# Operand slots of 4608 bytes with gaps, and matmuls row by row in the middle chunks

## The chip, the cores and the metric

One core of a Trainium2 chip runs one step of a decoder layer. The time is what the device needs for one execution, in microseconds (us). The engines are named as the profile names them: PE multiplies matrices (PEld is its loading of the stationary operand), DVE and ACT work element by element, POOL does a few element operations, SP issues the transfers.

## The reference

264 tokens (8 single decode tokens and a prompt of 256) go through one layer of width 2048:

```python
proj = rmsnorm(x) @ w_in          # 2048 -> 6144, split into u, v, q, k, v, g
out  = concat(u * spatial_mix(v), silu(g) * groupnorm(retention(q, k, v))) @ w_out
h = x + out
h = h + softmax(q @ mem_k.T) @ mem_v @ w_co     # q = rmsnorm(h) @ w_cq, 4 heads, 256 memory tokens
h = h + square(relu(rmsnorm(h) @ w_ff1)) @ w_ff2   # 2048 -> 8192 -> 2048
y = rmsnorm(h)
```

All of it is float32. The memory keys and values of the prompt are two more products (256 memory tokens by w_ck and w_cv), and the decode tokens attend to cached keys and values that are read from memory.

## The kernel before, in words

**Layout.** Activations lie transposed: 128 features down the partitions, the 264 tokens along them. A tile of four such blocks, [128, 4, 264], is a slot (`slot`, L46). All slots come from one pool of 26 equal buffers. A block of 264 tokens has 1056 bytes per partition, which is 4 x 256 + 32; a slot has 4 x 1056 = 4224 bytes, which is 16 x 256 + 128. In the built program the pool begins at byte 73,664 = 287 x 256 + 192 of the partition. I call the byte at which an operand begins, modulo 256, its **residue**. So a slot begins at residue 192 or 64, its four blocks follow in steps of 32, and before the change all eight multiples of 32 occur as residues.

**The product.** A float32 operand is split into a rounded part and the rest (`split`, L98; the activations' pairs are `xh`/`xl`, `h1h`/`h1l`, `rh`/`rl` and so on, made by `pair`, L502; the weights' are `wh`/`wl`). One product of 128 features by 128 outputs is then three matmuls (L152 to L154): `wh` with the high part, `wh` with the low part, `wl` with the high part. The weights are the stationary operand, and the 264 tokens of one block move through. I call such three matmuls a **turn**. A turn is named by m, which of four groups of 128 outputs and so which bank of the accumulator it goes to, and by k, which of two blocks of features.

**The stream.** The weights come as 512 chunks of 256 x 512 numbers in a fixed order (L979 to L1018). Each chunk is loaded (L1024), rounded on ACT (L1030) and subtracted on DVE (L1038), some two chunks ahead of its matmuls. `group_act` (L136) makes 476 of the chunks: 444 with 264 columns and 32 with 256 (the memory keys, L999). A group of 16 blocks has 8 chunks; one of the feed-forward's second product has 4. A chunk has 8 turns, so 24 matmuls. Their order is by m first: both k for one bank, then the next bank. Only the first three chunks (FINE) go by k first. `group_mem` (L163, 32 chunks, the memory values) has the weights as the moving operand, 512 columns; `group_last` (L110) is the last group of four chunks.

**Other work.** Everything else (norms, attention, gating) is written as generators that are advanced a step at a time between turns (`run_point`, L210), so it stands in the engines' queues in that order. In the attention of the decode tokens (L806) DVE multiplies a cached key or value by a broadcast query and adds up (L822, L845); the product itself goes to a scratch tile of the pool `half` (L58) that nobody reads, in turn one of three buffers.

Of the kernel before, what the change touches and what calls it, by code (L numbers as in the profile page):

```python
# [6 lines left out]
F32 = mybir.dt.float32  # L7
F32R = mybir.dt.float32r
# [4 lines left out]
T = 264  # L13
TOK = ((8, 128), (136, 128), (0, 8))
EPS = 1e-6
NSLOT = 26
# [4 lines left out]
FINE = 3  # L21
# [4 lines left out]
G_N1, G_SGU, G_GN, G_N2, G_MEM, G_N3, G_FIN = 0, 16, 24, 32, 48, 64, 80  # L26
GAMMA = [1.0 - 2.0 ** (-5 - h) for h in range(8)]
R4 = range(4)


def build(tc, I, O):
    cst = tc.tile_pool(name="cst", bufs=1)
    wpool = tc.tile_pool(name="wpool", bufs=1)
    spool = tc.tile_pool(name="spool", bufs=1)
    tpool = tc.tile_pool(name="tpool", bufs=1)
    psum = tc.tile_pool(name="psum", bufs=1, space=bass.MemoryType.PSUM)
    with cst as cst, wpool as wpool, spool as spool, tpool as tpool, psum as psum:
        with tc.manual_schedule():
            _emit(tc, cst, wpool, spool, tpool, psum, I, O)


def _emit(tc, cst, wpool, spool, tpool, psum, I, O):
# [3 lines left out]
    def slot(shape, name, dt=F32):  # L46
        return spool.tile(shape, dt, name=name, tag="s", bufs=NSLOT)

    def t264(name="t"):
        return tpool.tile([128, T], F32, name=name, tag="t", bufs=9)  # L50

# [4 lines left out]
        return tpool.tile([128, n], F32, name=name, tag="sm", bufs=24)  # L56

    def half(name, dt=F32):  # L58
        return tpool.tile([128, 512], dt, name=name, tag="hf", bufs=3)

    def bank(shape, name):
        return psum.tile(shape, F32, name=name, tag="mm", bufs=5)
# [4 lines left out]
    S = {}  # L67
# [6 lines left out]
        S.pop(key)  # L74
        S.pop(key + "_cm").__exit__(None, None, None)

# [1 line left out]
    cmat = cst.tile([128, 272], F32, name="cmat")  # L78
    ident, trilt = cmat[:, 0:128], cmat[:, 128:256]
    kdec = cmat[:, 256:272]  # L80
# [3 lines left out]
    sel = cst.tile([128, 8], F32R, name="sel")  # L84
# [3 lines left out]
    def gain(base, k):  # L88
        return gcol[:, base + k:base + k + 1]
# [8 lines left out]
    def split(hi, lo, src, scale=None):  # L98
        if scale is None:
            act.copy(hi, src)  # L100
            dve.tensor_tensor(out=lo, in0=src, in1=hi.bitcast(F32), op=ALU.subtract)
        else:
            act.activation(hi, src, AF.Copy, scale=scale)  # L103
            dve.scalar_tensor_tensor(out=lo, in0=src, scalar=scale, in1=hi.bitcast(F32),  # L104
                                     op0=ALU.mult, op1=ALU.subtract)

# [1 line left out]
    chunks, started = [], []  # L108

    def group_last(w, opnd, evict):  # L110
# [25 lines left out]
    def group_act(w, nk, opnd, evict, pre=None, rot=0, n=T):  # L136
        st = {}

        def mm(ci, hi, lo):
            if ci == 0:  # L140
                st["ps"] = [bank([128, n], "acc") for _ in R4]
            turns = [(m, k) for m in R4 for k in range(2)]
            if len(started) < FINE:
                started.append(1)
                turns.sort(key=lambda t: t[1])
            for j, (m, k) in enumerate(turns):
                i = 2 * ci + k
                xh, xl = opnd((i + rot) % nk)
                a = hi[:, k, m * 128:(m + 1) * 128]
                b = lo[:, k, m * 128:(m + 1) * 128]  # L150
                ps = st["ps"][m][:]
                pe.matmul(ps, lhsT=a, rhs=xh, start=(i == 0), stop=False)  # L152
                pe.matmul(ps, lhsT=a, rhs=xl, start=False, stop=False)  # L153
                pe.matmul(ps, lhsT=b, rhs=xh, start=False, stop=(i == nk - 1))  # L154
                if j % 2:
                    yield

        for ci in range(nk // 2):
            chunks.append(dict(
                src=w[(ci + rot // 2) % (nk // 2)], mm=mm, ci=ci, pre=pre[ci] if pre and ci in pre else None,  # L160
                post=(lambda: evict(st["ps"])) if ci == nk // 2 - 1 else None))
# [20 lines left out]
            chunks.append(dict(src=w[ci], mm=mm, ci=ci, pre=None,  # L182
                               post=(lambda: evict(st["ps"])) if ci == 7 else None))

# [1 line left out]
    tasks, chains = [], []  # L186
    stores = deque()
    now = [0]
# [41 lines left out]
            now[0] += 1  # L230
            run_point()

# [1 line left out]
    class Stats:  # L234
        def __init__(self, n=T):
            self.n = n
            self.acc = tpool.tile([128, n], F32, name="sq", tag="sq", bufs=2)
            self.first, self.tail, self.ps = True, None, None
# [63 lines left out]
    def opnd_of(tiles):  # L302
        return lambda kt: (tiles[kt // 4][0][:, kt % 4, :], tiles[kt // 4][1][:, kt % 4, :])

# [1 line left out]
    open_pool("rpool")  # L306
    dve.memset(ones[:, 0:128], 1.0 / 2048)
    dve.memset(ones[:, 128:256], 1.0)
# [17 lines left out]

    keep_warm(NWARM)

    A = [(slot([128, 4, T], "xh", F32R), slot([128, 4, T], "xl", F32R)) for _ in R4]
    st1 = Stats()  # L330

    def prep_x(s, ks=R4):
# [52 lines left out]
        dve.tensor_scalar(out=tab[:, 2:4, :], in0=tab[:, 0:2, :], scalar1=128.0 ** -0.5, scalar2=None, op0=ALU.mult)  # L385
        S["tab"] = tab

# [1 line left out]
    def normed(ps):  # L389
        z = [t264("z") for _ in R4]  # L390
        for m in R4:
# [108 lines left out]
            dve.tensor_tensor(out=dst[1][:, m, :], in0=src[m][:], in1=dst[0][:, m, :].bitcast(F32), op=ALU.subtract)  # L500

    def pair(name):  # L502
        return slot([128, 4, T], name + "h", F32R), slot([128, 4, T], name + "l", F32R)

    def ev_u(g):
        def ev(ps):
# [10 lines left out]
            chain(gen())  # L517
        return ev

# [1 line left out]
    def ev_rope(which, g):  # L521
        def ev(ps):
            o = slot([128, 4, T], which)
# [156 lines left out]
            chain(gen())  # L680
        return ev

# [1 line left out]
    def ev_res(g, dst, st, gbase, name):  # L684
        def ev(ps):
            if g == 0:
# [20 lines left out]
            chain(gen())  # L707
        return ev

# [1 line left out]
    memop = []  # L711

    def mem_load(s):
# [4 lines left out]
    def mem_prep():  # L718
        st = Stats(256)
        nxt = mem_load(0)  # L720
        yield 6
        for s in R4:
            t = nxt
            if s < 3:
                nxt = mem_load(s + 1)
            mh, ml = slot([128, 4, 256], "memh", F32R), slot([128, 4, 256], "meml", F32R)
            memop.append((mh, ml))
            for k in R4:
                split(mh[:, k, :], ml[:, k, :], t[:, k, :], gain(G_MEM, 4 * s + k))
                q = st.square(t[:, k, :])  # L730
                yield 2
                st.add(q)

        def fin():
            tok = ((0, 128), (128, 128))
            st.column(tok)
            yield 4
            S["rsmb"] = cst.tile([128, 256], F32, name="rsmb")
            st.spread(S["rsmb"][:], tok)
            S["rsm"] = st.col  # L740
        defer(fin(), 10, front=True)
# [14 lines left out]
    def ev_cq(h):  # L756
        def ev(ps):
            if h == 0:
                zt = half("zt")
                dve.memset(zt[:], 0.0)  # L760
                S["qs"] = S["mpool"].tile([128, 512], F32R, name="qs", tag="qs", bufs=1)
                S["pst"] = S["mpool"].tile([128, 256], F32R, name="pst", tag="pst", bufs=1)
                act.copy(S["qs"][:], zt[:])
                act.copy(S["pst"][:], zt[:, 0:256])
                kv_fill()
            z = [t264("z") for _ in R4]
            for m in R4:
                dve.tensor_tensor(out=z[m][:], in0=ps[m][:], in1=S["st2r"][:], op=ALU.mult)
            qh, ql = pair("q")
            qx.append((qh, ql))  # L770
            small8 = S["mpool"].tile([128, 4, 8], F32, name="q8", tag="q8", bufs=4)
            q8.append(small8)

            def gen():
                for m in R4:
                    act.copy(small8[:, m, :], z[m][:, 0:8])
                    act.copy(qh[:, m, :], z[m][:])
                yield 4
                for m in R4:
                    gp.tensor_tensor(out=ql[:, m, :], in0=z[m][:], in1=qh[:, m, :].bitcast(F32), op=ALU.subtract)  # L780
            chain(gen())
            defer(sample_attn(h), 4, lane="kv")
        return ev

    def join_o(h):
        if h in oT and h in oS:
            oh, ol = oT[h]
            split(oh[:, :, 0:8], ol[:, :, 0:8], oS[h][:])

    def softmax(s, n, then=None):  # L790
        mx, nb, sm, rc = small(1, "mx"), small(1, "nb"), small(1, "sm"), small(1, "rc")
# [12 lines left out]
        return ex  # L804

    def sample_attn(h):  # L806
        qs, pst = S["qs"], S["pst"]
        tp = misc([8, 512], "tp")
        for m in R4:
            transpose(tp[:, m * 128:(m + 1) * 128], q8[h][:, m, :])  # L810
# [27 lines left out]
        for b in range(8):  # L838
            kv_fill()
            vc = kvq.popleft()  # L840
            pb = misc([128, 256], "pb")
            pe.matmul(pb[:], lhsT=sel[:, b:b + 1].broadcast_to([128, 128]), rhs=pst[:], start=True, stop=True)
            for d in R4:
                jk = half("vjk")
                dve.scalar_tensor_tensor(out=jk[:, 0:256], in0=vc[:, d * 256:(d + 1) * 256], scalar=1.0, in1=pb[:],  # L845
                                         op0=ALU.mult, op1=ALU.mult, accum_out=so[:, d, b:b + 1])
            yield 4
            kv_fill()
# [72 lines left out]
            split(oh[:, d, 8:T], ol[:, d, 8:T], op[:])  # L921
            yield 2

# [1 line left out]
    ffb = {}  # L925

    def ev_ff1(b, g):
# [48 lines left out]
            S["st4"].tail = t  # L976
            act.activation(S["gh"][3], h, AF.Copy, scale=gain(G_FIN, 15))

# [1 line left out]
    order = [("q", 2048), ("k", 3072), ("v", 4096), ("q", 2560), ("k", 3584), ("v", 4608),  # L980
             ("vA", 1024), ("vA", 1536), ("g", 5120), ("g", 5632), ("u", 0), ("u", 512)]
    seen = {}
# [13 lines left out]
        group_act(I["w_cq"][g], 16, opnd_of(opc), ev_cq(g))  # L996
    n_cq = len(chunks)
    for h in R4:
        group_act(I["w_ck"][h], 16, opnd_of(memop), ev_mk(h), n=256)  # L999
        group_mem(I["w_cv"][h], opnd_of(memop), ev_mv(h))  # L1000
    n_mem = len(chunks)
    for g in R4:
        group_act(I["w_co"][g], 16, opnd_of(oT), ev_res(g, opd, "st3", G_N3, "h2"))
# [206 lines left out]
```

## Time and profile before

| | |
|---|---|
| time, median of 3 runs | 1607.97 us (1607.68 to 1608.06) |
| span of the profiled execution, first to last instruction | 1605.7 us |
| PE busy | 1589.0 us, 12608 matmuls |
| DVE busy | 1049.4 us |
| ACT busy | 743.9 us |
| POOL busy | 146.5 us |
| transfers | 326.15 MB, DMA engines busy 59.2% on the queue that carries them |

The profiled execution has no time of its own beside its span; the median of the runs is 2.3 us above that span, which is what lies before the first and behind the last instruction. Matmuls are pipelined, so the duration of one overlaps the next; what counts for the time is the distance from the start of one to the start of the next. The timeline gives starts to 0.01 us.

### The profile page before, as it was taken

The numbers are of one execution on the slowest core, as the hardware profiler recorded it, in microseconds if no ns is written. First come the engines' busy times: TensorE is split into PE (matmuls) and PEld (weight loads), VectorE is DVE, ScalarE is ACT, GpSimd is POOL, SyncE is SP. The second block draws the span as 40 slices with busy tenths as digits, with TensorE's granted clock in tenths as the row PEclk, the third lists the DMA queues.
The fourth block names the chain that finished last, engine by engine and source line by source line (L and its number), as shares of the span: only waits on it lengthen the run. The fifth ranks groups of instructions, "written<-read, shape, count | busy, mean of one in ns | idle before, by whom it ended". The sixth has DMA issues, their size and how long they took to land.

```text
span 1605.7 us, 31031 instructions
## 1 busy us (share of the span) xinstructions
PE 1589.0 (99%) x12608; PEld 1560.8 (97%) x12608; DVE 1049.4 (65%) x1897; ACT 743.9 (46%) x1156; POOL 146.5 (9%) x138
## 2 busy tenths in 40 slices
PE   8999999999999999999999999999999999999997
PEld 7999999999999998999999999999999999999997
DVE  8758688678668777877655554554655555565555
ACT  5445466357444444444545443534444353444432
POOL 7403022010012111001000000000000000000000
PEclk9999999999999999999999999999999999999999
DMA  7565655455578887877555555455555555555552
GB/s 262 184 224 197 218 175 194 143 189 208 192 250 284 311 311 284 275 277 255 177 184 175 180 171 196 172 182 186 172 186 171 195 172 186 182 180 187 172 185 80
DMA packets 94222, 326.15 MB, mean 203 GB/s; under 512 B 10608, under 2 KB 15344, under 8 KB 94080
## 3 DMA queue, kind: packets, MB, share of 16 engines
q1 hardware_dynamic: 94080, 324.18, 59.2%
q8 instruction: 98, 1.61, 0.4%
q14 instruction: 44, 0.36, 0.1%
HBM read 313.03 MB, written 11.11 MB: 202 GB/s over the span
## 4 chain that ended last, share of the span: by engine, by line
PE 96%; DVE 2%; DMA 0%; issue 0%; ACT 0%; SPq 0%; POOL 0%; DVEq 0%; ACTq 0%
PE acc L152 28%; PE acc L153 28%; PE acc L154 28%; PE acc L176 2%; PE acc L178 2%; PE acc L177 2%; PE tp L96 1%; DVE wl L1038 1%; PE qb L819 0%; DMA hT<-in_xT_dram 0%; PE bc L618 0%; DVE xl L104 0%; PE spp L482 0%; DVE y L1121 0%; PE rsb L290 0%
## 5 line engine op out<-in xcount | busy, mean ns | idle before, releaser
L1030 ACT CAST wh<-w 128x1024 fp32r<-128x1024 f32 (+1 forms) x513 | 536.3, 1046 | 721.6 <-PE acc L153 638.7
L1038 DVE TENSOR_TENSOR wl<-w,wh 128x1024 fp32r<-128x1024 f32 (+1 forms) x513 | 631.2, 1243 | 255.1 <-ACT wh L1030 254.4
L152 PE MATMUL acc<-h2h,wh 128*128 128x264 f32 x1024 | 291.1, 284 | 0.0
L153 PE MATMUL acc<-h2l,wh 128*128 128x264 f32 x1024 | 291.0, 284 | 0.0
L154 PE MATMUL acc<-h2h,wl 128*128 128x264 f32 x1024 | 290.9, 284 | 0.0
L153 PE MATMUL acc<-rl,wh 128*128 128x264 f32 x992 | 282.3, 285 | 0.0
L154 PE MATMUL acc<-rh,wl 128*128 128x264 f32 x992 | 282.1, 284 | 0.0
L152 PE MATMUL acc<-rh,wh 128*128 128x264 f32 x992 | 282.1, 284 | 0.0
L152 PE MATMUL acc<-xh,wh 128*128 128x264 f32 x768 | 225.4, 293 | 0.2
L154 PE MATMUL acc<-xh,wl 128*128 128x264 f32 x768 | 219.9, 286 | 3.5 <-DVE wl L1038 2.9
L153 PE MATMUL acc<-xl,wh 128*128 128x264 f32 x768 | 219.6, 286 | 0.0
L152 PEld LDWEIGHTS acc<-h2h,wh 128*128 128x128 f32 x1024 | 192.9, 188 | 0.0
L153 PEld LDWEIGHTS acc<-h2l,wh 128*128 128x128 f32 x1024 | 192.8, 188 | 0.0
L154 PEld LDWEIGHTS acc<-h2h,wl 128*128 128x128 f32 x1024 | 192.6, 188 | 0.0
L152 PEld LDWEIGHTS acc<-rh,wh 128*128 128x128 f32 x992 | 187.0, 189 | 0.0
L153 PEld LDWEIGHTS acc<-rl,wh 128*128 128x128 f32 x992 | 186.8, 188 | 0.0
L154 PEld LDWEIGHTS acc<-rh,wl 128*128 128x128 f32 x992 | 186.5, 188 | 0.0
L154 PEld LDWEIGHTS acc<-xh,wl 128*128 128x128 f32 x768 | 145.7, 190 | 4.4 <-DVE wl L1038 3.7
L152 PEld LDWEIGHTS acc<-xh,wh 128*128 128x128 f32 x768 | 145.7, 190 | 1.9 <-ACT xh L103 0.7
L153 PEld LDWEIGHTS acc<-xl,wh 128*128 128x128 f32 x768 | 145.8, 190 | 0.2 <-DVE xl L104 0.2
L950 DVE TENSOR_TENSOR hT<-hT,acc 128x264 f32<-128x264 f32 x124 | 53.3, 430 | 73.4 <-PE acc L154 73.4
L92 POOL TENSOR_TENSOR msr<-msv,neghalf 128x3 f32<-128x3 f32 (+1 forms) x5 | 7.8, 1551 | 944.9 <-DVE msv L265 738.6
(255 smaller groups left out, 2800.0 us busy)
## 6 DMA issues: line engine op xcount, KB each, us to landing
w<-in_w_ff_dram SPq DMA_DIRECT2D x256, 512.0 KB, 4.1
w<-in_w_in_dram SPq DMA_DIRECT2D x95, 512.0 KB, 3.9
w<-in_w_out_dram SPq DMA_DIRECT2D x32, 512.0 KB, 4.1
w<-in_w_cq_dram SPq DMA_DIRECT2D x32, 512.0 KB, 4.2
kv<-in_kN_dram SPq DMA_DIRECT2D x32, 512.0 KB, 4.9
kv<-in_vT_dram SPq DMA_DIRECT2D x32, 512.0 KB, 5.2
w<-in_w_ck_dram SPq DMA_DIRECT2D x32, 512.0 KB, 5.3
w<-in_w_cv_dram SPq DMA_DIRECT2D x32, 512.0 KB, 4.4
```

Of the source, the lines that this page charges most:

```text
L92: gp.tensor_tensor(out=out, in0=in_, in1=neghalf[0:in_.shape[0], 0:n], op=ALU.pow)
L96: pe.transpose(out, in_, ident[0:p, 0:p])
L152: pe.matmul(ps, lhsT=a, rhs=xh, start=(i == 0), stop=False)
L153: pe.matmul(ps, lhsT=a, rhs=xl, start=False, stop=False)
L154: pe.matmul(ps, lhsT=b, rhs=xh, start=False, stop=(i == nk - 1))
L176: pe.matmul(ps, lhsT=a, rhs=hi[:, k, :], start=(kt == 0), stop=False)
L177: pe.matmul(ps, lhsT=a, rhs=lo[:, k, :], start=False, stop=False)
L178: pe.matmul(ps, lhsT=b, rhs=hi[:, k, :], start=False, stop=(kt == 15))
L950: dve.tensor_tensor(out=h[m], in0=h[m], in1=ps[m][:], op=ALU.add)
L1030: act.copy(hi[:, k, :], raws[i][:, k, :])
L1038: dve.tensor_tensor(out=lo[:, k, :], in0=raw[:, k, :], in1=hi[:, k, :].bitcast(F32), op=ALU.subtract)
```

## The change

It has two parts and some room-making.

**Slots.** A slot becomes 4608 bytes (18 x 256). Tiles that are moving operands of `group_act` are now made by `rows`: the tile is [128, 2, 576], two stretches of 2304 bytes (9 x 256), each holding two blocks of 264 tokens one behind the other with 48 numbers unused. The class `Rows` shows it to the rest of the kernel under the old indices. A tile of 96 bytes is put ahead of the slots, so that they begin at 73,664 + 96 = 288 x 256 + 32. Every even block then has residue 32 and every odd one 64, in all these slots. The memory operands (256 columns) take the same form. Other tiles in slots (the residual, the memory values, the keys of the prompt's attention) keep their shapes.

**Order.** In the chunks of a group that are neither its first nor its last, the turns go by k first: four banks with one block, then four banks with the other. Which block is first alternates from chunk to chunk, so that one chunk ends and the next begins with the same k. In the first and last chunk of a group the order stays by m, with the two k swapped for every second m. The flags that open and close an accumulation follow.

**Room.** The slots need 26 x 384 + 96 bytes more. `half` goes from three buffers to one, and the tile `pst` (the spread probabilities) is gone: it now lies in the first half of `qs`.

```diff
+class Rows:
+    def __init__(self, t):
+        self.v = t[:, :, 0:2 * T].rearrange("p a (b t) -> p a b t", b=2)
+    def __getitem__(self, at):
+        p, k, c = at
+        if isinstance(k, int):
+            return self.v[p, k // 2, k % 2, c]
+        return self.v[p, :, :, c]
...
+    spool.tile([128, 24], F32, name="pad", tag="pad", bufs=1)
+    def rows(name):
+        return Rows(spool.tile([128, 2, 576], F32R, name=name, tag="s", bufs=NSLOT))
...
     def half(name, dt=F32):
-        return tpool.tile([128, 512], dt, name=name, tag="hf", bufs=3)
+        return tpool.tile([128, 512], dt, name=name, tag="hf", bufs=1)
...
-            turns = [(m, k) for m in R4 for k in range(2)]
-            if len(started) < FINE:
+            ks = (0, 1) if ci % 2 == 0 else (1, 0)
+            if len(started) < FINE or 0 < ci < nk // 2 - 1:
                 started.append(1)
-                turns.sort(key=lambda t: t[1])
+                turns = [(m, k) for k in ks for m in R4]
+            else:
+                turns = [(m, k) for m in R4 for k in (ks if m % 2 == 0 else ks[::-1])]
             for j, (m, k) in enumerate(turns):
                 i = 2 * ci + k
+                left = [t for t in turns[j + 1:] if t[0] == m]
+                begins, ends = ci == 0 and len(left) == 1, ci == nk // 2 - 1 and not left
...
-                pe.matmul(ps, lhsT=a, rhs=xh, start=(i == 0), stop=False)
+                pe.matmul(ps, lhsT=a, rhs=xh, start=begins, stop=False)
                 pe.matmul(ps, lhsT=a, rhs=xl, start=False, stop=False)
-                pe.matmul(ps, lhsT=b, rhs=xh, start=False, stop=(i == nk - 1))
+                pe.matmul(ps, lhsT=b, rhs=xh, start=False, stop=ends)
...
-    A = [(slot([128, 4, T], "xh", F32R), slot([128, 4, T], "xl", F32R)) for _ in R4]
+    A = [(rows("xh"), rows("xl")) for _ in R4]
...
     def pair(name):
-        return slot([128, 4, T], name + "h", F32R), slot([128, 4, T], name + "l", F32R)
+        return rows(name + "h"), rows(name + "l")
...
-            mh, ml = slot([128, 4, 256], "memh", F32R), slot([128, 4, 256], "meml", F32R)
+            mh, ml = pair("mem")
...
-        qs, pst = S["qs"], S["pst"]
+        qs, pst = S["qs"], S["qs"][:, 0:256]
```

More of the change, by code (lines that the diff above doesn't have):

```diff
@@ L303, in opnd_of, with opnd_mem @@
         return lambda kt: (tiles[kt // 4][0][:, kt % 4, :], tiles[kt // 4][1][:, kt % 4, :])
+    def opnd_mem(kt):
+        return tuple(t[:, kt % 4, 0:256] for t in memop[kt // 4])
     open_pool("rpool")
@@ L725, in mem_prep @@
                 nxt = mem_load(s + 1)
-            mh, ml = slot([128, 4, 256], "memh", F32R), slot([128, 4, 256], "meml", F32R)
+            mh, ml = pair("mem")
             memop.append((mh, ml))
             for k in R4:
-                split(mh[:, k, :], ml[:, k, :], t[:, k, :], gain(G_MEM, 4 * s + k))
+                split(mh[:, k, 0:256], ml[:, k, 0:256], t[:, k, :], gain(G_MEM, 4 * s + k))
                 q = st.square(t[:, k, :])
@@ L761, in ev @@
                 S["qs"] = S["mpool"].tile([128, 512], F32R, name="qs", tag="qs", bufs=1)
-                S["pst"] = S["mpool"].tile([128, 256], F32R, name="pst", tag="pst", bufs=1)
                 act.copy(S["qs"][:], zt[:])
-                act.copy(S["pst"][:], zt[:, 0:256])
                 kv_fill()
@@ L787, in join_o @@
             oh, ol = oT[h]
-            split(oh[:, :, 0:8], ol[:, :, 0:8], oS[h][:])
+            split(oh[:, :, 0:8], ol[:, :, 0:8], oS[h][:].rearrange("p (a b) t -> p a b t", a=2))
     def softmax(s, n, then=None):
@@ L841, in sample_attn @@
             pb = misc([128, 256], "pb")
-            pe.matmul(pb[:], lhsT=sel[:, b:b + 1].broadcast_to([128, 128]), rhs=pst[:], start=True, stop=True)
+            pe.matmul(pb[:], lhsT=sel[:, b:b + 1].broadcast_to([128, 128]), rhs=pst, start=True, stop=True)
             for d in R4:
@@ L998, in _emit @@
     for h in R4:
-        group_act(I["w_ck"][h], 16, opnd_of(memop), ev_mk(h), n=256)
-        group_mem(I["w_cv"][h], opnd_of(memop), ev_mv(h))
+        group_act(I["w_ck"][h], 16, opnd_mem, ev_mk(h), n=256)
+        group_mem(I["w_cv"][h], opnd_mem, ev_mv(h))
     n_mem = len(chunks)
```

## The prediction

> **What bounds the kernel now.** I read the page first, then the chain that ended last, then windows, then the timeline of PE.
>
> ```profile
> span 1605.7 us, 31031 instructions
> PE 1589.0 (99%) x12608; PEld 1560.8 (97%) x12608; DVE 1049.4 (65%) x1897; ACT 743.9 (46%) x1156; POOL 146.5 (9%) x138
> PEclk9999999999999999999999999999999999999999
> PE 96%; DVE 2%; DMA 0%; issue 0%; ACT 0%; SPq 0%; POOL 0%; DVEq 0%; ACTq 0%
> ```
>
> PE is busy for 1589 of 1605.7 us, its clock is granted in full, and 96% of the chain that ended last is PE. No transfer and no other engine stands in its way, so only two things can move the time: fewer matmuls (the change keeps them all) or a shorter distance between their starts. That distance is the subject. The next view gives the busy time in three stretches. In the first two the PE count is 384 matmuls that begin inside (16 chunks) and some that overlap the edges.
>
> ```profile
> core 0: us, PE busy (x) PEld busy (x) DVE busy (x) ACT busy (x) POOL busy (x), PEclk, DMA share, GB/s
> 1030.74:1077.68 46.94, 46.94 (x386) 46.94 (x385) 27.24 (x36) 19.68 (x24) 0.00 (x0) 1.00 0.55 180
> 1217.88:1264.50 46.62, 46.62 (x387) 46.62 (x386) 27.23 (x36) 19.70 (x24) 0.00 (x0) 1.00 0.55 181
> 466.00:748.00 282.00, 282.00 (x1969) 263.01 (x1969) 222.89 (x569) 125.30 (x189) 40.71 (x32) 1.00 0.83 291
> ```
>
> Both upper stretches do the same work with the same DVE and ACT load, at 46.94 / 384 = 122.2 ns and 46.62 / 384 = 121.4 ns. What differs is where their operands lie. By the program's allocation the first has high and low part 128 bytes apart modulo 256 (residues 64 and 192, or 128 and 0), the second has both parts at one residue (64 with 96 for the next block, or 128 with 160). So the address counts, but here for only 0.7%.
>
> Inside one chunk of the second stretch, the first matmul of each turn:
>
> ```profile
> 1229.54 0.28 PE L152 MATMUL acc<-rh,wh 128*128 128x264 f32 x1
> ...
> 1229.89 0.28 PE L152 MATMUL acc<-rh,wh 128*128 128x264 f32 x1
> ...
> 1230.26 0.28 PE L152 MATMUL acc<-rh,wh 128*128 128x264 f32 x1
> ...
> 1230.62 0.29 PE L152 MATMUL acc<-rh,wh 128*128 128x264 f32 x1
> ...
> 1230.99 0.28 PE L152 MATMUL acc<-rh,wh 128*128 128x264 f32 x1
> ...
> 1231.35 0.28 PE L152 MATMUL acc<-rh,wh 128*128 128x264 f32 x1
> ...
> 1231.72 0.28 PE L152 MATMUL acc<-rh,wh 128*128 128x264 f32 x1
> ...
> 1232.08 0.29 PE L152 MATMUL acc<-rh,wh 128*128 128x264 f32 x1
> ...
> 1232.44 0.28 PE L152 MATMUL acc<-rh,wh 128*128 128x264 f32 x1
> ```
>
> The turns alternate between residue 64 and residue 96. The four at 64 take 0.35 + 0.36 + 0.36 + 0.36 = 1.43 us (357.5 ns each), the four at 96 take 1.47 us (367.5). So one residue, entered from another, differs from its neighbour by 10 ns in a turn.
>
> **The change part by part.** The same count over the whole trace needs classes of turns, from start to start, leaving out the turns that a wait or another matmul interrupts. These are the first and last turns of the classes:
>
> ```profile
> 6.66 0.28 PE L152 MATMUL acc<-xh,wh 128*128 128x264 f32 x1
> ...
> 340.96 0.28 PE L152 MATMUL acc<-mgh,wh 128*128 128x264 f32 x1
> ...
> 341.69 0.28 PE L152 MATMUL acc<-mgh,wh 128*128 128x264 f32 x1
> ...
> 344.25 0.28 PE L152 MATMUL acc<-mgh,wh 128*128 128x264 f32 x1
> ...
> 441.28 0.29 PE L152 MATMUL acc<-h1h,wh 128*128 128x264 f32 x1
> ...
> 442.02 0.28 PE L152 MATMUL acc<-h1h,wh 128*128 128x264 f32 x1
> ...
> 1567.79 0.28 PE L152 MATMUL acc<-rh,wh 128*128 128x264 f32 x1
> ...
> 1569.97 0.28 PE L152 MATMUL acc<-rh,wh 128*128 128x264 f32 x1
> ...
> 1578.36 0.28 PE L152 MATMUL acc<-rh,wh 128*128 128x264 f32 x1
> ...
> 1578.72 0.28 PE L152 MATMUL acc<-rh,wh 128*128 128x264 f32 x1
> ```
>
> - All turns (3335, from 6.66 to 1578.72): mean 365.1 ns, 121.7 per matmul; the shortest is 350, the longest 381.
> - Both parts at residue 64, the block before it 32 bytes further on (129 turns, 442.02 to 1569.97): 359.2.
> - Both at 32 (181 turns, 344.25 to 1578.36), always entered from a block 32 bytes lower: 363.9.
> - Same residue within the turn, entered by a step back of 32 (528, 341.69 to 1578.72): 362.7; by a step forward of 32 (840, 340.96 to 1578.36): 365.8.
> - Residue 64 entered from 32 (33 turns, 441.28 to 1567.79): 373.5.
>
> *Term A, the residues.* After the change half of the turns lie at 32 and half at 64, both parts alike. At today's prices that is (359.2 + 363.9) / 2 = 361.55, so 3.55 ns less in each of 444 x 8 = 3552 turns: -12.6 us.
>
> *Term B, fewer steps.* Today every turn enters a new residue. Afterwards a middle chunk has one step in eight turns, and none to the next chunk; a first or last chunk has four. The trace has no undisturbed long run at one residue with 264 columns, so the price of "no step" is bounded by the cheap and the dear step, 362.7 and 365.8. The turns at 32 are all of the dear kind today. I credit them half the difference: 1.55 x 1776 = -2.8 us; the bounds are 0 and -5.5 us.
>
> *Term C, the steps that stay.* Of the 444 chunks 302 are middle ones (240 of 320 in the groups of eight, 62 of 124 in the groups of four). They make 151 forward steps from 32 to 64 and as many back; the other 142 chunks make two of each, 284. The forward step is one that the trace shows to be dear: 373.5 - 359.2 = 14.3 ns, times 435 is +6.2 us. But these 33 turns come from few places in the program, and a common forward step costs 365.8 - 362.7 = 3.1 ns, +1.3 us. I take +3 us.
>
> *Operands with 256 and 512 columns.* The memory keys (768 matmuls) move from residues 64 and 192 to 32 and 64. No row shows them there; I give them 0, with the difference of the two windows, 0.8 ns x 768 = 0.6 us, as the bound either way. The memory values have weights as moving operand, whose place does not change: 0.
>
> *The first chunks.* Chunk 1 now begins with its second block, whose weights are rounded second.
>
> ```profile
> 11.08 0.40 PE L154 MATMUL acc<-xh,wl 128*128 128x264 f32 x1 [0.58 <-DVE wl L1038]
> 16.62 0.47 PE L154 MATMUL acc<-xh,wl 128*128 128x264 f32 x1 [2.36 <-DVE wl L1038]
> 9.96 2.23 DVE L1038 TENSOR_TENSOR wl<-w,wh 128x512 fp32r<-128x512 f32 x2
> ```
>
> The matmul that waits until 11.08 would wait until 9.96 + 2.23 = 12.19, 1.1 us more. But chunk 2 is held by DVE until 16.62 after 2.36 us of idling, so the delay is covered: 0. Without that cover it would be +1.1 us.
>
> *One scratch tile for three.* Each product on DVE into the scratch tile must now follow the one just before it, not the third before.
>
> ```profile
> 520.72 0.42 DVE L845 SCALAR_TENSOR_TENSOR vjk<-kv,pb 128x256 f32<-128x256 f32 x1 [0.46 <-PE pb L842]
> 521.06 0.41 DVE L845 SCALAR_TENSOR_TENSOR vjk<-kv,pb 128x256 f32<-128x256 f32 x1
> ```
>
> They start 0.34 us apart and last 0.42, so strict order costs at least 0.08 us for each of 128 + 64 of them, 15 us of DVE time. The stretch 466 to 748 has 282 - 222.9 = 59 us of DVE idle. Behind them in DVE's queue stands the subtraction for a chunk two ahead (5.8 us at 24 x 121.7 ns), so four of them make it late by 0.3 us and PE does not see it: 0. Without that cover it would be up to +15 us. The shared `qs` adds no wait either: the copy that overwrites it follows a transpose that stands behind its last reader in PE's own queue. Evictions keep their place, since the last chunk of a group still finishes bank by bank.
>
> The sum: -12.6 - 2.8 + 3 = -12.4 us against the profiled span of 1605.7, so 1593.3, and with the 2.3 us around it **1596 us**.
>
> [...]
>
> **The rivals.**
>
> *Long runs lock at a better pace than anything averaged so far.* With 12 turns at one residue in a row, each could cost what the best of today cost: 357.5 for the four at 64 above gives 7.6 x 3552 = -27 us, 1581; the shortest turn of all, 350, gives -54 us, 1554. For it: the intervals repeat exactly where the addresses do. Against it: the best turns sit next to dear ones, so part of their gain may be borrowed. I price it at 1575.
>
> *The long run is the slow case*, the one that ends on the other side. The trace has one kind of run without steps, with 256 columns, where both parts and all blocks lie at residue 192:
>
> ```profile
> 549.68 0.28 PE L152 MATMUL acc<-memh,wh 128*128 128x256 f32 x1
> ...
> 551.84 0.39 PE L819 MATMUL qb<-qs,sel 128*128 128x512 f32 x1
> 564.09 0.40 PE L176 MATMUL acc<-wh,memh 128*128 128x512 f32 x1
> ...
> 565.97 0.40 PE L178 MATMUL acc<-wh,meml 128*128 128x512 f32 x1
> ```
>
> Its 18 starts lie 2.16 / 18 = 120.0 ns apart, and the 8 with 512 columns lie 235 apart. The slope, 115 / 256 = 0.449 ns per column, makes 123.6 ns of 264 columns, 1.9 more than today's 121.7. If that is what a run at one residue costs, the middle chunks lose 302 x 24 x 1.9 = +13.8 us: 1622. It decides as soon as the run's pace lies above 121.7. Against it: a block of 264 ends 32 bytes behind where one of 256 ends, so the next start stands otherwise to the end before it.
>
> *The address hardly counts*, or the slots do not begin where the change says: every pattern of today that I can set side by side lies between about 121 and 123 ns, and new ones may just fall in the middle: 1608, give or take 3.
>
> **How the numbers follow.** The forecast of 1596 gets 0.46, with its own range from 1591 (B at its bound, common steps, 256 columns better: -17.4) to 1602 (B zero, all forward steps dear, 256 columns worse: -5.8). The better lock gets 0.22, the slower run 0.18, no effect 0.14. A measurement of this kernel tells about 0.2%, 3.2 us, from no change; so faster has 0.46 + 0.22 = 0.68, same 0.14, slower 0.18. The range reaches into both outer cases, 1570 to 1618.
>
> **What would show it.** Right: in the feed-forward stage 24 matmuls in about 2.89 us instead of 2.91, turns at 64 near 359 and at 32 near 362 ns, PE still at 99%, and no new wait in its list. A is wrong if residues 32 and 64 no longer differ from the 365.1 of all; B if the second to fourth turn of a run are no cheaper than the first; C if the step from 32 to 64 shows as a turn of 373 in every chunk. The prediction falls if middle chunks cost more than 2.92 us, if they fall below 2.85, or if PE begins to wait for `wl` in the attention stage.

## The result and the profile after

The changed kernel takes 1619.97 us (1619.43 to 1620.11, 4 runs) where the kernel before takes 1608.01 us (1607.68 to 1608.45): a ratio of 1.0074, 95% interval 1.0061 to 1.0087. It is slower by 12 us; the forecast was 1596.

The page of the changed kernel, its first lines:

```profile
span 1617.6 us, 31030 instructions
PE 1598.1 (99%) x12608; PEld 1569.3 (97%) x12608; DVE 1060.0 (66%) x1897; ACT 743.0 (46%) x1155; POOL 146.4 (9%) x138
PEclk9999999999999999999999999999999999999999
```

As before, PE is busy for 99% of the span, at a mean granted clock of 0.998 (0.997 before). So the 11.9 us by which the span grew are once more a matter of the distance between starts. A window of 400 us, most of it in the feed-forward stage, where all but 12 of PE's matmuls are products with 264 columns, shows it. First the kernel before, then the changed one (the bracket behind PE is the number of matmuls in the window):

```profile
800.00:1200.00 400.00, 400.00 (x3288) 399.86 (x3287) 224.00 (x289) 175.56 (x227) 1.77 (x1) 1.00 0.54 180
```

```profile
800.00:1200.00 400.00, 400.00 (x3262) 399.77 (x3261) 222.88 (x286) 173.54 (x225) 1.77 (x1) 1.00 0.56 178
```

400 us / 3288 is 121.7 ns from start to start, 400 / 3262 is 122.6; in the timeline below a single matmul lasts 0.28 to 0.29 us, so they overlap. Over the whole trace, leaving out intervals that a wait interrupts, the mean of 264 columns went from 121.70 ns (10,632 intervals) to 122.67 (10,650): 0.97 x 10,650 = 10.3 of the 11.9 us. The same window serves below as the measure of each experiment.

Inside the changed order, the first matmul of each turn (the timeline of the changed kernel):

```profile
1148.63 0.29 PE L174 MATMUL acc<-rh,wh 128*128 128x264 f32 x1
...
1151.56 0.28 PE L174 MATMUL acc<-rh,wh 128*128 128x264 f32 x1
...
1153.41 0.29 PE L174 MATMUL acc<-rh,wh 128*128 128x264 f32 x1
```

From 1148.63 eight turns run at residue 32 through two chunks and take 2.93 us, 366 ns each; the five at residue 64 that follow take 1.85 us, 370 ns each. I had expected 362 and 359.

What PE waited for, the longest rows of the list of the changed kernel:

```profile
PE acc L176 <- DVE wl L1061: 4.4, 3, 1.7
PE rsb L312 <- DVE dg L308: 1.7, 2, 1.0
PE acc L174 <- ACT xh L121: 1.2, 1, 1.2
```

All three waits for `wl` lie in the first 25 us, and chunk 12 begins at 51.65 us for 51.18 before. No wait of the attention stage joined the list.

### The profile page after: what moved, and what is told of

Same layout as the page of the kernel before. It is cut to its first block, busy times and chain, and to the rows that moved or that the text cites. A ratio compares the mean times of both kernels' runs of the same rounds, so it can differ in the third digit from the quotient of the medians.

```text
span 1617.6 us, 31030 instructions
## 1 busy us (share of the span) xinstructions
PE 1598.1 (99%) x12608; PEld 1569.3 (97%) x12608; DVE 1060.0 (66%) x1897; ACT 743.0 (46%) x1155; POOL 146.4 (9%) x138
## 4 chain that ended last, share of the span: by engine, by line
PE 57%; DVE 1%; issue 0%; POOL 0%; ACT 0%; DVEq 0%; ACTq 0%
PE acc L176 18%; PE acc L174 18%; PE acc L175 18%; PE acc L199 1%; PE acc L198 1%; PE acc L200 1%; DVE wl L1061 0%; DVE y L1144 0%; PE acc L144 0%; PE acc L143 0%; PE acc L142 0%; PE qb L842 0%; PE rsb L312 0%; PE sc L918 0%; PE sc L920 0%
```

## The experiments

Where an experiment changes residues only, the weights (the stationary operand) stay at residue 192 as in both kernels.

**The two parts of the change, one at a time.** The first kernel has the slots alone:

```diff
-            ks = (0, 1) if ci % 2 == 0 else (1, 0)
-            if len(started) < FINE or 0 < ci < nk // 2 - 1:
+            turns = [(m, k) for m in R4 for k in range(2)]
+            if len(started) < FINE:
                 started.append(1)
-                turns = [(m, k) for k in ks for m in R4]
-            else:
-                turns = [(m, k) for m in R4 for k in (ks if m % 2 == 0 else ks[::-1])]
+                turns.sort(key=lambda t: t[1])
```

> The slots of 4608 bytes stay (residues 32 and 64), the turns go back to the old order: by m first, k inside. Three theories of the 12 us. Residues: any turn at 32 or 64 with both parts alike costs about 368 ns, in whatever order; then about 1620. Runs: what costs is the long run at one residue; here each turn steps, as in the edge chunks of the changed kernel, so about 1610 to 1614. Banks: what costs is the change of the accumulator's bank at every turn; the old order changes it at every second, so 1608.

The second has the order alone: the same lines the other way round, with the flags, in the kernel before.

> The slots go back to 4224 bytes and all eight residues, the row order of the changed kernel stays. Residues: about 1608, as only the addresses count. Runs: about 1615 to 1620, since a row now repeats for four turns at any residue, though six in ten chunks have the two parts 128 bytes apart. Banks: about 1618 to 1620, the whole loss.

Slots alone: 1626.51 us (1626.11 to 1626.94), ratio 1.0114 (1.0099 to 1.0129). Order alone: 1607.12 us, ratio 0.9994 (0.9985 to 1.0004). The window of 800 to 1200 us, slots alone and then order alone:

```profile
800.00:1200.00 400.00, 400.00 (x3242) 399.74 (x3242) 221.19 (x285) 173.75 (x225) 1.77 (x1) 1.00 0.55 177
```

```profile
800.00:1200.00 400.00, 400.00 (x3289) 399.86 (x3288) 224.03 (x288) 174.99 (x228) 1.77 (x1) 1.00 0.57 180
```

So the loss is the slots'. They cost 18.5 us, and the new order takes 6.5 of these back; with the old slots the order is worth nothing that can be told. Runs at one residue are not slow in themselves here: the order alone has them, of four turns each, at all eight residues, and stays at 121.6 ns. Runs of eight turns, as the changed kernel has them, come with the experiments below.

**What a residue costs in a long run.** To price residues by themselves, runs of matmuls were appended behind the last instruction of the kernel before. They are extra work and the whole time says nothing; what counts is the distance of starts inside each run. Each of the two sets of such runs was executed once.

```diff
+    def run(name, turns, n=T): ...      # turns of wh·high, wh·low, wl·high into 4 banks
+    for j in range(8):                  # A: moving parts 32 bytes further on for each j
+        run(f"A{j}q", [(wt(t % 4), t % 4, 8 * j, 8 * j + LSH) for t in range(16)])
...
+    for j in range(8):                  # H: moving parts fixed, weights 32 bytes further on
+        run(f"H{j}q", [((Z2[:, 8 * j + 128 * (t % 4):...], ...), t % 4, 8, 8 + LSH) for t in range(16)])
```

> The kernel before, with runs of 16 turns of matmuls appended behind its end, which write to accumulator banks that nobody reads (the time is that of the appended work, too; only the distances of starts count). A0 to A7: one bank per turn, both parts at one residue, 192 + 32 j modulo 256. B: the same with the bank changed every second turn. C: two rows alternate, 1056 bytes apart, bank every second turn. D: as A with the low part 128 bytes further. E: as A with 256 columns. F0 to F63: as A in steps of 4 bytes, 8 turns. G: one set of weights for all turns. H: other addresses of the weights. Residues: A and B alike, A3 (32) and A4 (64) near 122.7 ns per matmul and the others lower, near 121. Runs: A and B near 122.7 for every j, C near 121.7. Banks: A near 122.7, B near 121.5, whatever j.

The timeline has, first and last, the first matmul of a turn for four of these runs (they stand 15 turns, 45 matmuls, apart). A4 has the moving operands at residue 64 and the weights at 192, A6 at 128 and 192, H1 at 224 and 96, H5 at 224 and 224:

```profile
1634.05 0.29 PE L1142 MATMUL A4q<-pz,pw 128*128 128x264 f32 x1
...
1639.60 0.29 PE L1142 MATMUL A4q<-pz,pw 128*128 128x264 f32 x1
...
1645.82 0.28 PE L1142 MATMUL A6q<-pz,pw 128*128 128x264 f32 x1
...
1651.24 0.28 PE L1142 MATMUL A6q<-pz,pw 128*128 128x264 f32 x1
...
2042.29 0.28 PE L1142 MATMUL H1q<-pz,pq 128*128 128x264 f32 x1
...
2047.84 0.29 PE L1142 MATMUL H1q<-pz,pq 128*128 128x264 f32 x1
...
2065.72 0.28 PE L1142 MATMUL H5q<-pz,pq 128*128 128x264 f32 x1
...
2071.12 0.28 PE L1142 MATMUL H5q<-pz,pq 128*128 128x264 f32 x1
```

5.55 us / 45 is 123.3 ns for A4 and for H1, 5.42 / 45 is 120.4 for A6, 5.40 / 45 is 120.0 for H5. A4 and H1 share no residue, only the distance from stationary to moving operand: 64 - 192 and 224 - 96 are both 128 modulo 256. Set side by side by this **difference**, the two sets agree but for difference 0, where a second run of A gave 120.0 too (settled pace in ns, the mean over the last three quarters of a run):

| moving - stationary mod 256 | 0 | 32 | 64 | 96 | 128 | 160 | 192 | 224 |
|---|---|---|---|---|---|---|---|---|
| moving operand shifted (A) | 121.4 | 122.2 | 120.9 | 121.7 | 123.3 | 121.7 | 120.0 | 120.0 |
| weights shifted (H) | 120.0 | 122.2 | 121.0 | 121.7 | 123.3 | 121.7 | 120.0 | 120.0 |

The change puts the operands at differences 96 and 128, which make (121.7 + 123.3) / 2 = 122.5 ns; the changed kernel's turns inside a run measure 367.5 / 3 = 122.5. That the means agree is partly luck: by residue these turns measure 368.1 / 3 = 122.7 at 32 (1183 turns) and 366.8 / 3 = 122.3 at 64 (1158), where the runs have 121.7 and 123.3. The runs A with the bank changed every second turn (B) gave the same numbers within 0.1 ns, so the order of the banks plays no part in them. One set of weights for all turns (G) gave 122.2, as A1 has at the same residues, so new weights in every turn are not what costs there. In set C both parts alternate between two blocks 32 bytes apart; there the pair 32/64 was the worst of all at 124.4 ns. The slots alone have this pattern, and average 123.4.

**The same slots, moved.** In the next two kernels the changed kernel's blocks begin 96 and 160 bytes further on inside their slots, at residues 128/160 and 192/224 (differences 192/224 and 0/32):

```diff
-        self.v = t[:, :, 0:2 * T].rearrange("p a (b t) -> p a b t", b=2)
+        self.v = t[:, :, 24:24 + 2 * T].rearrange("p a (b t) -> p a b t", b=2)   # and 40:40 + 2 * T
```

> The changed kernel with its blocks 96 bytes further into the slots: residues 128 and 160 in place of 32 and 64; order, slot size and weights (residue 192) as changed. By the appended runs of the probe (A6 and A7 settle at 120.0 ns, C6 too, against 121.7 in the kernel before): -1.7 ns x 10650 = -18 us on 1608, about 1590. If the size of the slots or the row order were what costs, it stays at about 1620.

> As e3 with residues 192 and 224, so that blocks and weights begin at equal residues or 32 apart. By the probe (A0 121.4 or, once, 120.0; A1 122.2) about 121.5 ns, so 1604 to 1608. If only the slots' size counted: 1620.

128/160 (e3): 1603.08 us, ratio 0.9969 (0.9957 to 0.9980). 192/224 (e4): 1606.35 us, ratio 0.9988 (0.9978 to 0.9997). Both go the right way, 17 and 14 us below the change. But 128/160 misses the 1590 of the run prices by 13 us. Its turns show where 10 of them are: 340 turns at 128 that stand before a step forward take 376.6 ns where 840 inside a run take 362.8 (+4.7 us), 464 that enter by that step 367.2 where turns inside a run at 160 take 359.9 (+3.4 us), and the 840 lie 2.8 ns above the 360 of the run prices (+2.4 us). So run prices hold inside runs to about 1 ns per matmul, and a step between blocks has a price of its own, in the turn before it as well as in the one behind it.

**The weights moved instead.** The sharpest test of the difference keeps the changed kernel's own residues 32 and 64 and moves the weights from 192 to 96, which makes the differences 192 and 224:

```diff
-    spool.tile([128, 24], F32, name="pad", tag="pad", bufs=1)
+    cst.tile([128, 40], F32, name="pad")                       # ahead of the weights
...
-        self.v = t[:, :, 0:2 * T].rearrange("p a (b t) -> p a b t", b=2)
+        self.v = t[:, :, 48:48 + 2 * T].rearrange("p a (b t) -> p a b t", b=2)
...
-        return tpool.tile([128, n], F32, name=name, tag="sm", bufs=24)
+        return tpool.tile([128, n], F32, name=name, tag="sm", bufs=23)
```

> The blocks stay at the residues 32 and 64 of the changed kernel, the weights' tiles move from residue 192 to 96 (one small ring of buffers has 23 in place of 24, to make room). Two theories. Difference: what counts is the moving operand's residue minus the stationary one's; it becomes 192 and 224 modulo 256, as in e3, so about 1590. Own place: what counts is the residue of the moving operand itself; then 1620 as in the changed kernel.

1603.07 us (1602.48 to 1604.91), ratio 0.9970 (0.9959 to 0.9981); turns at the two blocks take 365.1 and 361.8 ns, to the tenth what 128/160 gave. The window:

```profile
800.00:1200.00 400.00, 400.00 (x3302) 399.69 (x3301) 224.38 (x286) 175.75 (x228) 1.77 (x1) 1.00 0.57 182
```

3302 matmuls for the change's 3262, with moving operands at the same residues, the same order and the same slot size. The residue of the moving operand by itself did not cause the loss; where it lies against the weights did. These 17 us (1619.97 to 1603.07) were won by moving the weights alone; by what mechanism is not shown.

**Steps of 4 bytes.** The first appended set also had the moving operand in 64 places 4 bytes apart. Three neighbours, at residues 28, 32 and 36, first and last turn of 8:

```profile
1910.30 0.29 PE L1142 MATMUL F23q<-pz,pw 128*128 128x264 f32 x1
...
1912.79 0.28 PE L1142 MATMUL F23q<-pz,pw 128*128 128x264 f32 x1
...
1913.15 0.28 PE L1142 MATMUL F24q<-pz,pw 128*128 128x264 f32 x1
...
1915.70 0.29 PE L1142 MATMUL F24q<-pz,pw 128*128 128x264 f32 x1
...
1916.06 0.29 PE L1142 MATMUL F25q<-pz,pw 128*128 128x264 f32 x1
...
1918.71 0.29 PE L1142 MATMUL F25q<-pz,pw 128*128 128x264 f32 x1
```

2.49, 2.55 and 2.65 us over 21 intervals: 118.6, 121.4 and 126.2 ns. Grouped by residue modulo 16, the settled pace is 120.9 for 0 (16 places, 119.9 to 122.2), 124.3 for 4 (120.0 to 126.7), 123.3 for 8 (120.0 to 125.0) and **120.0 for 12** (118.7 to 121.8, 14 of the 16 at 119.9 or 120.0).

This set also shows that the addresses do not fix the pace by themselves. F32 lies where A4 lay, at residue 64 with the weights at 192, and has the same order. These are the first matmuls of its third and of its last turn, 15 matmuls apart:

```profile
1937.41 0.28 PE L1142 MATMUL F32q<-pz,pw 128*128 128x264 f32 x1
...
1939.21 0.28 PE L1142 MATMUL F32q<-pz,pw 128*128 128x264 f32 x1
```

1.80 / 15 is 120.0 ns, where A4 settled at 123.3. The two runs differ in the run that stands before them, in the banks that they were given and in their length; which of these decides is not shown. The same holds for difference 0, at 121.4 or 120.0 above.

A second set of appended runs asked what this depends on.

```diff
+    for j in range(64):                 # I: moving at residue 32, weights in steps of 4 bytes
+        run(f"I{j}q", [(wt(t % 4, j), t % 4, 24, 24 + LSH) for t in range(8)])
+    for j in range(64):                 # K: moving at residue 28, weights in steps of 4 bytes
+        run(f"K{j}q", [(wt(t % 4, j), t % 4, 23, 23 + LSH) for t in range(8)])
...                                      # J: other orders in a turn; N, P: other column counts
```

> The kernel before with other runs of matmuls appended behind its end, which write to accumulator banks that nobody reads; only the distances of starts count. A: as A of the first probe, as a control, with the weights in a slot at residue 192: the same by residue if the first probe's pattern is the addresses'. I and K: weights shifted in 64 steps of 4 bytes under fixed blocks (residues 32 and 28): by the difference theory the pace varies as much as it did when the blocks were shifted; by the own-place theory it is constant. J and M: other orders and subsets of the three matmuls of a turn, at residues 64 and 160. [...] R: random offsets of high part, low part and weights.

With the moving operand at residue 32, the 64 places of the weights give anything from 119.8 to 126.7 ns; at residue 28 they give 118.7 to 122.2, and 60 of the 64 at most 120.5. One pair from each, at residues 32 and 28, and both with the difference 244:

```profile
1736.44 0.28 PE L1146 MATMUL I27q<-pz,pv 128*128 128x264 f32 x1
...
1739.34 0.28 PE L1146 MATMUL I27q<-pz,pv 128*128 128x264 f32 x1
...
1919.07 0.28 PE L1146 MATMUL K26q<-pz,pv 128*128 128x264 f32 x1
...
1921.83 0.28 PE L1146 MATMUL K26q<-pz,pv 128*128 128x264 f32 x1
```

2.90 / 23 = 126.1 ns and 2.76 / 23 = 120.0. So in steps of 4 bytes the difference alone is not the rule, and at residue 28, 12 bytes behind a multiple of 16, the place of the weights moves the pace by 3.5 ns at most (by 6.9 at residue 32).

The 48 random places (R) add a condition. With both parts at 12 modulo 16, four of five runs settled at 120.0 ns and one at 121.1; with the high part alone there, 13 runs gave 120.0 to 124.4. In the kernels below both parts lie alike.

Whether the order within a turn counts is not shown. At residue 64, `wh`·high, `wl`·high, `wh`·low settles at 120.0 ns, but so does F32 with the kernel's order, and both begin with the same six distances, 123, 116, 122, 123, 122 and 118 ns. `wh`·low, `wh`·high, `wl`·high settles at 123.3, as A4 does. In all three orders the moving parts repeat as high, high, low. No kernel was run with another order inside the turn.

**Kernels at 12 modulo 16.** Four kernels use this. The first three shift the blocks inside the changed kernel's slots: by 27 numbers (residues 140/172), by 3 (44/76), and by 27 with the old order. The fourth is the kernel before with every moving operand 12 bytes into a slot of 4240 bytes, so all eight residues, each 12 higher, and a scratch pool of two buffers.

```diff
-        self.v = t[:, :, 0:2 * T].rearrange("p a (b t) -> p a b t", b=2)
+        self.v = t[:, :, 27:27 + 2 * T].rearrange("p a (b t) -> p a b t", b=2)   # or 3:3 + 2 * T
```

```diff
+    def rows(name, n=T):                                       # the fourth, in the kernel before
+        t = spool.tile([128, 1060], F32R, name=name, tag="s", bufs=NSLOT)
+        return t[:, 3:3 + 4 * n].rearrange("p (k t) -> p k t", k=4)
```

> The changed kernel with the blocks 108 bytes further on inside their slots, so at residues 140 and 172 (12 modulo 16); the order stays the changed one. In the probe that moved the operand in steps of 4 bytes nearly every run at a residue of 12 modulo 16 went at 120.0 ns. Sixteen-byte theory (the start modulo 16 decides, wherever the weights lie): 120.0 ns for the 10,650 undisturbed matmuls against 121.18 at residues 128/160, so -12.6 us from 1603.1: 1590, span 1588. Theory of the difference alone (140 - 192 and 172 - 192 lie in the same cheap half as 128 and 160): 1603, pace 121.2. If a step between blocks costs what it cost at 128/160 whatever the residue, half of the gain: 1597.

> The changed kernel with the blocks only 12 bytes further on, residues 44 and 76, order unchanged. Difference theory: the difference to the weights hardly moves (108 and 140 for 96 and 128), so the loss stays: 1617 to 1621, pace 122.5. Sixteen-byte theory: 120.0 ns, -2.67 ns on 10,650 matmuls = -28 us: 1592. Between them, if steps keep their price: 1600.

> Residues 140 and 172 with the old order (by m, a step between blocks in every turn). With residues 32/64 this order cost 1626.5 where the changed one cost 1620.0. Sixteen-byte theory: no residue of 12 modulo 16 is dear and a step costs nothing, so 1590, the same as the other order. If steps have a price of their own that long runs save: +6 us, 1596 to 1609.

> The kernel before, old order, slots of 4240 bytes and every moving operand 12 bytes into its slot, so that all eight residues occur as before, each 12 higher (12, 44, ... 236); nothing else of the change except that the scratch pool has two buffers instead of three. Sixteen-byte theory: 120.0 ns against 121.70, -18 us from 1608: 1590. Difference theory: the mix over all eight differences stays, 1608. If only runs at one residue gain: 1605 to 1608.

| kernel | residues | order | time, us | ratio to before (95%) | mean of 264 columns, ns |
|---|---|---|---|---|---|
| before | all eight | old | 1608 | 1 | 121.70 |
| changed | 32/64 | new | 1619.97 | 1.0074 (1.0061 to 1.0087) | 122.67 |
| e6 | 140/172 | new | 1600.88 | 0.9955 (0.9939 to 0.9971) | 120.92 |
| e7 | 44/76 | new | 1595.57 | 0.9922 (0.9906 to 0.9938) | 120.33 |
| e8 | 140/172 | old | 1608.17 | 1.0000 (0.9990 to 1.0010) | 121.65 |
| e9 | all eight + 12 | old | 1599.42 | 0.9946 (0.9930 to 0.9962) | 120.93 |

12 bytes turn the change's loss of 12 us into a gain of 12.4 (e7). The window of e7:

```profile
800.00:1200.00 400.00, 400.00 (x3324) 399.68 (x3324) 224.82 (x286) 176.63 (x228) 1.77 (x1) 1.00 0.58 183
```

e7 confirms in a kernel that the difference alone is not the rule: by that theory 108 and 140 should have stayed near the loss. But "12 modulo 16 makes 120.0 everywhere" was too much too. e6 came out at 120.92, since 172 is the one such place that had 121.8 in its run (its turns here take 364.7 ns, those at 140 take 360.8). e8 gained nothing: in the old order every turn at 140 and 172 is a step, and costs 364.1 and 365.8. e9 won 8.8 of the 18 us, with the steps kept.

**Four bytes lower.** The last kernel puts the blocks at residues 28 and 60, 4 bytes below the change's own:

```diff
-        self.v = t[:, :, 0:2 * T].rearrange("p a (b t) -> p a b t", b=2)
+        self.v = t[:, :, 7:7 + 2 * T].rearrange("p a (b t) -> p a b t", b=2)
...
-    spool.tile([128, 24], F32, name="pad", tag="pad", bufs=1)
+    spool.tile([128, 16], F32, name="pad", tag="pad", bufs=1)
```

> The changed kernel with every block 4 bytes lower than the change puts it: residues 28 and 60 instead of 32 and 64 (slots begin 32 bytes lower and the blocks 28 bytes into them); order and everything else unchanged. The difference to the weights is 92 and 124 for 96 and 128. Difference theory: the loss stays, 1616 to 1621. Sixteen-byte theory: both are 12 modulo 16, so as at 44 and 76: 1594 to 1597. If the lower pace of the probe at residue 28 (118.67 ns instead of 120.0) holds in half of the turns, -1.3 ns on some 5300 matmuls, -7 us from 1595.6: 1589.

1592.58 us (1591.81 to 1593.29), ratio 0.9902 (0.9886 to 0.9919): 27.4 us below the changed kernel and 15.4 below the one before, the fastest of all (its interval overlaps that of e7). The window, and the timeline of a run at residue 28:

```profile
800.00:1200.00 400.00, 400.00 (x3332) 399.67 (x3331) 224.49 (x286) 177.04 (x229) 1.77 (x1) 1.00 0.57 184
```

```profile
1155.00 0.28 PE L174 MATMUL acc<-rh,wh 128*128 128x264 f32 x1
...
1157.49 0.28 PE L174 MATMUL acc<-rh,wh 128*128 128x264 f32 x1
```

Seven turns in 2.49 us are 355.7 ns each, 118.6 per matmul, as in the run at residue 28 above. All turns at 28 average 356.5 ns (1681 turns), those at 60 363.5, 1.2 ns per matmul more than their run had.

## Why the prediction was wrong

- *What bounds the kernel* was right: PE stayed at 99% at a granted clock of 0.998, and 10.3 of the 11.9 us are in the distance between starts of the 264-column products.
- *Term A, the residues (-12.6 us)*, is the step that failed, and it carries nearly the whole miss. It took 359.2 ns for a turn at 64 and 363.9 at 32 from turns that each stood between steps, and applied them to runs. Measured, inside a run: 367.5 (2342 turns at 32 and 64, each entered from a turn at its own residue). 367.5 - 361.55, times 3552 turns, is +21.1 us; the span came out 24.3 above the forecast's 1593.3. A turn's price between two steps is partly its neighbours': 64 took 359.2 entered from 96 and 373.5 from 32. The two prices came from entries that the changed kernel does not have: 64 was entered from 96, and 32 from 0. The one step into 64 that it does have, from 32, stood among my rows, and where that pattern comes back its price does too: in the kernel with the slots alone the 1633 turns at 64 take 373.1. I also read the residue as a property of the moving operand, since the weights lay at 192 throughout the trace of before. That was wrong, but it did not make this miss, because they lie at 192 in the changed kernel too.
- *Term B, fewer steps (-2.8)* had the right sign: turns inside a run measure 367.5 ns (2342), those entered by a step 368.7 forward (465) and 370.1 back (479). The larger evidence is slots alone against the changed kernel, where the order saves 6.5 us. By the kernels at 140/172 (1608.17 against 1600.88) it saves 7.3.
- *Term C, the steps that stay (+3)*: a forward step costs 368.7 - 367.5 = 1.2 ns more, and a step back 2.6; that is 0.6 + 1.2 = +1.8 us for the turns counted here, where B and C together had +0.2. With A's 21.1 that explains 22.7 of the 24.3 us. The 14.3 ns that bounded the forward step came back only in part: the 69 turns at 64 that are entered from 32 and left again at once take 373.1, the others that are entered so 367.9.
- *256 columns (0)*: 118.7 to 119.1 ns over the undisturbed intervals of the 768 matmuls, some +0.3 us; within its bound of 0.6. *First chunks (0)*: 0.47 us later at chunk 12; right within half a microsecond, though PE's waits for `wl` grew from 3.3 to 4.4 us.
- *One scratch tile (0)*: right. In the stretch from 466 to 748 us DVE's busy time grew by 8.4 us and PE's fell by 0.4:

```profile
466.00:748.00 282.00, 281.59 (x1954) 261.78 (x1954) 231.26 (x557) 123.94 (x188) 39.70 (x34) 1.00 0.83 289
```

- *The rivals.* "The long run is the slow case" named 1622, close to the time, but its mechanism is refuted: order alone, which has runs of four turns, is not slower, the kernel at 44/76, which has runs of eight, is faster, and slots alone, which has none, is the slowest kernel of all. It extended one run (256 columns, residue and weights both at 192) along a straight line in columns; in the appended runs the pace is no straight line (below). "A better lock" named 1575: a run at the best of today's pace (357.5 ns a turn) exists, at residue 28 (355.7), but not in the changed kernel at 32 or 64 (367.5). "The address hardly counts" is refuted: from slots alone to the last kernel, addresses and order make 34 us. In the appended runs 264 columns settled at 118.7 to 126.7 ns, at a granted clock of 1.00 as in this window, which holds A4:

```profile
1634.00:1640.00 6.00, 6.00 (x51) 6.00 (x50) 0.00 (x0) 0.00 (x0) 0.00 (x0) 1.00 0.00 0
```

What stays open is the mechanism. Nothing here shows why a difference of 128 is dear, why the same addresses can have two settled paces, or why 12 modulo 16 is good; and the price of a step between blocks was seen (it took 8 us from the kernel at 128/160) but not derived.

## What to carry to other kernels

Here, with PE busy for 99% of the span at a granted clock of 0.997 to 0.998, the place of the moving operand, modulo 16 and against the weights modulo 256, was worth 1.7% (1619.97 to 1592.58 us for 4 bytes), and it cost a few bytes to change. A price read off a pattern that alternates belongs to that pattern: a turn at 64 took 359.2 ns there and 366.8 in a run. Runs of the very pattern wanted, appended to the kernel, tell more, but they missed one kernel by 13 us (1603.08 for 1590) and gave two prices for one place (123.3 and 120.0 ns), so the kernel itself has to decide. And before crediting an address with an effect, ask which other address never moved in the trace.

## What was not expected of the hardware

- The pace of the 264-column matmuls changed with where moving and stationary operand begin relative to each other: 120.0 to 123.3 ns in steps of 32 bytes modulo 256 (A, H), and 17 us of a kernel for the weights' place alone (1619.97 to 1603.07). It is not fixed by that: at the difference 128 runs settled at 123.3 (A4, H1) and at 120.0 (F32, I56).
- It changed with the moving operand's start modulo 16: with high and low part alike (F), 120.0 ns on average at 12 (118.7 to 121.8) and 124.3 at 4 (120.0 to 126.7).
- The pace by columns is no line in these runs. At residue 64 (P, for 264 columns A): 111.7 ns for 240 as for 128 columns, 118.9 for 256, 123.3 for 264, 126.7 for 272 and 133.2 for 288; at 128 (N, for 264 A) it is 113.3, 120.0, 123.3 and 133.5 for 256, 264, 272 and 288. These are single runs, and the first set had 117.8 for 256 columns at 128 (E6), so the place alone does not fix these either. The rows at residue 64 for 256 and for 224 columns:

```profile
2128.52 0.28 PE L1146 MATMUL P7q<-pz,pv 128*128 128x256 f32 x1
...
2131.25 0.28 PE L1146 MATMUL P7q<-pz,pv 128*128 128x256 f32 x1
...
2144.98 0.27 PE L1146 MATMUL P10q<-pz,pv 128*128 128x224 f32 x1
...
2147.55 0.27 PE L1146 MATMUL P10q<-pz,pv 128*128 128x224 f32 x1
```

2.73 / 23 is 118.7 ns (118.9 once settled) and 2.57 / 23 is 111.7.
